# The order of a whole two-block transformer kernel, listed with another machine model of the framework

## Chip, cores and metric

One core of a Trainium2 chip. The metric is the device time of one execution in microseconds (us). Matmuls run on PE (with the weight loads, PEld, beside it), elementwise work on DVE, ACT and POOL; SP issues most of the loads from memory.

## What is computed

Two transformer blocks over 256 tokens of width 1024, one after the other, in float32. Cut to what matters here:

```python
def first_block(x, mem, ...):
    h = rms_norm(x, mix_norm_pre)
    q, kc, vc, ksl, vsl, kw, vw, gt, pin, u, v = split(h @ w_in)
    mix = concat([nsa_mixer(q, kc, ...), pool_mixer(pin, ...), sgu_mixer(u, v, ...)]) @ w_out
    x = x + rms_norm(mix, mix_norm_post)
    x = x + rms_norm(memory_attention(rms_norm(x), rms_norm(mem), ...))
    return x + rms_norm(conv_ffn(rms_norm(x), w_up, conv_w, w_down))

def second_block(x, mem, ...):
    qkv, z, a_g, b_g, c_q, c_kv, k_idx, w_idx, ug = split(rms_norm(x, norm_mix) @ w_in)
    y_a = gdn_mixer(qkv, z, a_g, b_g, ...)      # gated delta rule: solves (I + A) sol = rhs, A strictly lower
    y_b = dsa_mixer(c_q, c_kv, k_idx, w_idx, ...)  # scores, top-k, attention over the chosen keys
    y_c = conv_mixer(ug, conv_dw, ...)          # 31-tap causal depthwise convolution, layer norm
    x = x + concat([y_a, y_b, y_c]) @ w_out
    x = x + memory_cross_attention(rms_norm(x), rms_norm(mem), ...)
    return x + square(relu(rms_norm(x) @ mlp_w1)) @ mlp_w2
```

## The kernel before

All activations stay on the core; the weights are streamed. A weight tile of 128x1024 (512 KB) is loaded on SP (`load_w`, L207), and split into a rounded high part on ACT (`wh`, L220) and a remainder on DVE in two halves (`wl`, L222; some tiles on POOL, L227 and L228). Each product is three matmuls (`mm3`, L232 to L234: high by high, high by low, low by high). Results lie in PSUM tiles of three tags: `tp` (four buffers), `cc` and `fl` (two each).

The stages follow each other in `build` (L1644): the mixers of block 1, 0 to 179 us of the profile; the attention to memory, 179 to 290; the convolutional FFN, 290 to 447, and its last product, to 491; the mixers of block 2, to 670; the cross attention, to 714; the MLP, to 893.

Two of these stages mix chains of small dependent steps with plain projections, called filler here, by Python generators that are run in turn (`weave`, L77, and `beside`, L97):

- Block 1. `nsa` (L655) works on two halves of the tokens, i = 0 and 1, with eight units in each: a score matmul L740 into `tp`, a bias and row minimum on DVE, an exponential on ACT, transposes L751, a copy, and the matmul with the values L762 into `cc`. The transposes of the result are L306. `fill1` (L780) gives the filler: the projections of the memory's keys and values (tiles `fl`), the pooling and the gating mixer. `w_out` (tiles `cc`) comes after all of it.
- Block 2. `gdn` (L1306) needs the inverse of a unit triangular matrix per head, which `tri_inverse` (L1366) builds: L1386 on DVE starts it from `ti_m` (POOL, L1385), and then six levels follow, each of them transposes L1380 (copied by ACT, L1381), matmuls L1395 (copied by ACT, L1396), matmuls L1401 and an update on DVE, L1402, for two halves i. `dsa` (L1407) has the second small chain: the keys and values (L1433, copied by ACT, L1435), scores L1465, a loop of MAX and MATCH_REPLACE on DVE (L1479, L1481) that finds the top-k, and a softmax (L1494 to L1512). `conv31` (L1520) is a chain of taps on DVE, one L1527 each, with nothing else to wait for than its input `yg`; `conv_silu` (L1078) has the taps L1086 of a shorter convolution, copied in by ACT L1084. `rest2` (L1250) and `fill2` (L1156) give the filler (tiles `fl`).

None of this fixes the order on the engines. The code hands its instructions to the framework's `TileContext`. When the context ends, the framework walks through a model of the machine and lists each engine's instructions in the order in which they become ready in that model; among ready ones the earlier in the code goes first. The list is the program: each engine works through it in that order. The model by default is the one with which the framework also computes values. The waits between engines, and the places of the table loads on ACT, follow from the list.

```python
x, hT, ss = ...                       # stages call weave / beside, e.g. L642:
weave((self.nsa(w1, x2, qT, kT, vsw, gate, mixT), NW), (self.fill1(hT, mixT, x2), FW))
```

The function that the change touches:

## Time and profile before

| | us |
|---|---|
| median of three runs | 893.49 |
| lowest and highest of them | 891.78, 899.03 |
| the profiled execution, its own time | 895.26 |
| its span on the core | 893.0 |
| mean granted clock of TensorE | 0.983 of full |

The span is the stretch that the profile's rows cover; 2.3 us of the execution lie around it. Times in rows count from the start of the span.

### The profile page before, as it was taken

What the parts mean: (1) busy time and instruction counts of PE and PEld (TensorE: products, weight loads), DVE (VectorE), ACT (ScalarE), POOL (GpSimd) and SP (SyncE); (2) the same over time, 40 slices, a digit from 0 to 9 for tenths busy, and PEclk for the clock granted to TensorE, in tenths of its full rate; (3) what the DMA queues carried; (4) which work ended last, traced back from release to release, by engine and by line L of the source; (5) the groups of instructions that cost most, each with busy time, mean ns of one, the idle gap of its engine ahead of it and who ended that gap; (6) DMA issues with size and microseconds to landing.
All of it is one profiled execution on the core that took longest, in us unless ns stands there. A gap on an engine that the chain in (4) does not pass through costs nothing.

```text
span 893.0 us, 15247 instructions
## 1 busy us (share of the span) xinstructions
PE 853.7 (96%) x5813; PEld 776.2 (87%) x5813; DVE 622.1 (70%) x1404; ACT 463.1 (52%) x805; POOL 118.0 (13%) x125
## 2 busy tenths in 40 slices
PE   8899999988999999999999997989999999999998
PEld 7798877888888999999988996878898999999996
DVE  5568765656557878877775799987666766666663
ACT  5346454545554656655554664656555534444442
POOL 1324101221110000000002312621142000000000
PEclk9989999999899999999999998999999999999999
DMA  8995223567343666765541652202153355666661
GB/s 256 278 285 170 72 76 117 163 190 236 119 156 117 200 212 211 226 191 181 189 139 57 201 150 96 88 1 95 28 162 95 105 180 174 186 186 190 187 188 70
DMA packets 41012, 138.94 MB, mean 156 GB/s; under 512 B 4851, under 2 KB 6292, under 8 KB 40940
## 3 DMA queue, kind: packets, MB, share of 16 engines
q1 hardware_dynamic: 37440, 130.49, 46.6%
q10 hardware_dynamic: 2988, 6.06, 2.2%
q0 software_dynamic: 512, 1.44, 0.9%
q8 instruction: 45, 0.74, 0.3%
q14 instruction: 27, 0.22, 0.1%
HBM read 136.00 MB, written 1.44 MB: 154 GB/s over the span
## 4 chain that ended last, share of the span: by engine, by line
PE 71%; DVE 16%; DMA 5%; ACT 4%; issue 3%; POOL 1%; ACTq 0%; SPq 0%; POOLq 0%; DVEq 0%
PE tp L234 8%; PE tp L233 8%; PE tp L232 8%; PE fl L232 6%; PE fl L233 5%; PE fl L234 5%; PE cc L234 4%; PE cc L233 4%; PE cc L232 4%; DVE wl L222 3%; DVE cv_y L1527 2%; DMA wr<-in_w_in_dram 2%; PE tp L331 1%; PE cc L762 1%; DMA srow<-in_srows_dram 1%
## 5 line engine op out<-in xcount | busy, mean ns | idle before, releaser
L222 DVE TENSOR_TENSOR wl<-wr,wh 128x512 fp32r<-128x512 f32 (+2 forms) x418 | 281.3, 696 | 130.2 <-ACT wh L220 128.2
L220 ACT ACTIVATE wh<-wr 128x1024 fp32r<-128x1024 f32 (+2 forms) x209 | 217.8, 1044 | 198.8 <-PE tp L233 87.7
L232 PE MATMUL tp<-thi,wh 128*128 128x256 f32 x784 | 222.8, 284 | 2.5 <-ACT wh L220 2.5
L234 PE MATMUL tp<-thi,wl 128*128 128x256 f32 x784 | 222.7, 284 | 0.2 <-DVE wl L222 0.2
L233 PE MATMUL tp<-tlo,wh 128*128 128x256 f32 x784 | 222.7, 284 | 0.0
L232 PEld LDWEIGHTS tp<-thi,wh 128*128 128x128 f32 x784 | 150.6, 192 | 4.0 <-ACT wh L220 2.7
L233 PEld LDWEIGHTS tp<-tlo,wh 128*128 128x128 f32 x784 | 150.5, 192 | 1.3
L234 PEld LDWEIGHTS tp<-thi,wl 128*128 128x128 f32 x784 | 150.6, 192 | 0.4 <-DVE wl L222 0.4
L228 POOL TENSOR_TENSOR wl<-wr,wh 128x1024 fp32r<-128x1024 f32 (+2 forms) x21 | 49.9, 2382 | 298.1 <-ACT wh L227 295.0
L227 ACT ACTIVATE ff_h<-ff_y 128x256 fp32r<-128x256 f32 x54 | 22.2, 416 | 45.0 <-PE fl L234 42.1
L232 PE MATMUL fl<-thi,wh 128*128 128x256 f32 x144 | 42.6, 296 | 0.8 <-ACT wh L227 0.7
L232 PE MATMUL cc<-wh,ff_h 128*128 128x512 f32 x108 | 42.4, 392 | 0.9 <-ACT ff_h L227 0.9
L983 DVE SCALAR_TENSOR_TENSOR ff_y<-tp,col,ff_y 128x255 f32<-128x255 f32 x88 | 42.0, 477 | 0.8 <-ACT ff_y L981 0.6
L234 PE MATMUL cc<-wh,ff_h 128*128 128x512 f32 x108 | 42.4, 393 | 0.0
L233 PE MATMUL cc<-wl,ff_h 128*128 128x512 f32 x108 | 42.2, 391 | 0.0
L234 PE MATMUL fl<-wh,ff_h 128*128 128x512 f32 x108 | 42.2, 391 | 0.0
L233 PE MATMUL fl<-wl,ff_h 128*128 128x512 f32 x108 | 42.2, 391 | 0.0
L232 PE MATMUL fl<-wh,ff_h 128*128 128x512 f32 x108 | 42.1, 390 | 0.0
L233 PE MATMUL fl<-tlo,wh 128*128 128x256 f32 x144 | 41.7, 290 | 0.0
L234 PE MATMUL fl<-thi,wl 128*128 128x256 f32 x144 | 41.7, 289 | 0.0
L227 ACT ACTIVATE wh<-wr 128x1024 fp32r<-128x1024 f32 (+3 forms) x23 | 22.5, 984 | 22.2 <-DMA wr<-in_w_in_a_dram 4.9
L228 DVE TENSOR_TENSOR ff_h<-ff_y,ff_h 128x256 fp32r<-128x256 f32 x54 | 22.5, 422 | 14.9 <-ACT ff_h L227 14.9
(523 smaller groups left out, 1822.7 us busy)
## 6 DMA issues: line engine op xcount, KB each, us to landing
wr<-in_mlp_w_dram SPq DMA_DIRECT2D x64, 512.0 KB, 3.6
wr<-in_w_up_dram SPq DMA_DIRECT2D x44, 512.0 KB, 3.7
wr<-in_w_in_dram SPq DMA_DIRECT2D x31, 512.0 KB, 4.5
wr<-in_w_down_dram SPq DMA_DIRECT2D x22, 512.0 KB, 4.3
wr<-in_w_out_dram SPq DMA_DIRECT2D x16, 512.0 KB, 3.6
grow<-in_rows_dram ACTq DMA_DIRECT2D x8, 512.0 KB, 6.1
wr<-in_w_mk_dram SPq DMA_DIRECT2D x8, 512.0 KB, 3.6
wr<-in_w_mv_dram SPq DMA_DIRECT2D x8, 512.0 KB, 3.6
```

What stands on the lines that cost most here:

```text
L220: nc.scalar.activation(hi, raw, AF.Copy)
L222: nc.vector.tensor_tensor(lo[:, q], raw[:, q], hi[:, q].bitcast(F32), op=ALU.subtract)
L227: nc.scalar.activation(hi, raw, AF.Copy)
L228: (eng or nc.vector).tensor_tensor(lo, raw, hi.bitcast(F32), op=ALU.subtract)
L232: nc.tensor.matmul(out, a[0], b[0], start=first, stop=False)
L233: nc.tensor.matmul(out, a[0], b[1], start=False, stop=False)
L234: nc.tensor.matmul(out, a[1], b[0], start=False, stop=last)
L331: nc.tensor.matmul(pt[:, j * P:(j + 1) * P], xg[n][:, j * P:(j + 1) * P], dg, start=True, stop=True)
L762: nc.tensor.matmul(out[:, h * 64:(h + 1) * 64], pT[:, (e * (i + 1) + b) * P:(e * (i + 1) + b + 1) * P], vsw[b][:, vo:vo + 64], start=(b == ...
L983: nc.vector.scalar_tensor_tensor(y[:, e, k:], a[:, :S - k], self.c("conv_w", 44 * (2 - k) + c), y[:, e, k:], op0=ALU.mult, op1=ALU.add)
L1527: nc.vector.scalar_tensor_tensor(y[:, c, k:], yg[:, c, :S - k], self.c("conv_dw", 2 * (30 - k) + c), y[:, c, k:], op0=ALU.mult, op1=ALU.add)
```

## The change

One argument. The list of every engine is now made with the framework's timeline model of the machine in place of its model that computes values. No line that issues an instruction is edited.

```diff
-    with _tile.TileContext(nc) as tc:
+    with _tile.TileContext(nc, schedule_with_timeline_sim=True) as tc:
```

What the program holds is the same: 5351 instructions of PE with its waits left aside, 1388 of DVE, 128 of POOL and 260 of SP, each with the same operands. ACT has two more table loads, 20 for 18, since they stand wherever the next function needs another table. On PE nothing moves in the FFN (290 to 446 us) and nothing after the first 20 us of the MLP. The largest moves are in the mixers of block 1 (up to 41 us of the profile before) and of block 2 (up to 20 us).

Three places are shown. The first is DVE in the mixers of block 2, just ahead of the start of the triangular inverse, L1386 (`ds_cur` is the top-k loop's score tile, `cv_y` the sum of the convolution's taps). Before:

```order
L1474 TENSOR_TENSOR ds_cur_5876<-ds_cur_5876,con 128x128
L1086 SCALAR_TENSOR_TENSOR kq_5402<-fl_5944,col,kq_5402 128x255
L1229 SCALAR_TENSOR_TENSOR bq_1084_5927<-tp_6016,gd_dd_5922,t_1030_5711 128x128
...
L1086 SCALAR_TENSOR_TENSOR kq_5402<-fl_5944,col,kq_5402 128x253
L1479 MAX ds_m_1102_6032<-ds_cur_6030 128x8
L1386 TENSOR_TENSOR t_1030_5711<-con,ti_m_6044 128x512
L1481 MATCH_REPLACE ds_cur_6034<-ds_m_1102_6032,ds_cur_6030 128x128
L1386 TENSOR_TENSOR t_1030_5711<-con,ti_m_6053 128x512
```

The same place now:

```order
L1527 SCALAR_TENSOR_TENSOR cv_y_5401<-yg_5273,col,cv_y_5401 128x226
L1086 SCALAR_TENSOR_TENSOR kq_5402<-fl_5944,col,kq_5402 128x253
L1535 TENSOR_SCALAR cv_y_5401<-cv_y_5401,col 128x256
L1086 SCALAR_TENSOR_TENSOR vT_5403<-fl_6090,col,vT_5403 128x255
...
L1229 SCALAR_TENSOR_TENSOR bq_1084_5927<-tp_6025,gd_dd_5922,t_1030_5711 128x128
L1386 TENSOR_TENSOR t_1030_5711<-con,ti_m_6044 128x512
...
L1386 TENSOR_TENSOR t_1030_5711<-con,ti_m_6053 128x512
L1444 TENSOR_SCALAR ds_k_5557<-cc_5844,col 64x256 x2
L1453 TENSOR_SCALAR ds_sv_5858<-cc_5853 128x8
```

Now all 60 taps L1527 stand ahead of L1386, before 36 of them did, and the top-k loop, which had begun ahead of it, follows it.

The second place is PE in the same stage, from the start of the triangular inverse on (`fl_6262` is filler). Before:

```order
L1380 MATMUL tp_6056<-con,t_1030_5711 128x128 x4
L1395 MATMUL tp_6076<-t_1030_5711,ti_m_6074 128x128 x4
L1395 MATMUL tp_6084<-t_1030_5711,ti_m_6082 128x128 x4
L1401 MATMUL tp_6169<-t_1030_5711 128x128 x4
L1401 MATMUL tp_6175<-t_1030_5711 128x128 x4
L233 MATMUL fl_6262<-tlo_5075,wh_6265 128x256
...
L1395 MATMUL tp_6252<-t_1030_5711,ti_m_6250 128x128 x4
L233 MATMUL fl_6262<-tlo_5075,wh_6296 128x256
```

The same place now:

```order
L1442 MATMUL cc_5844<-con,ds_kn_5848 128x128
L1451 MATMUL cc_5853<-con,ds_pr_5798 128x2 x4
L1380 MATMUL tp_6047<-con,t_1030_5711 128x128 x4
...
L1401 MATMUL tp_6175<-t_1030_5711 128x128 x4
L1380 MATMUL tp_6181<-con,t_1030_5711 128x128 x4
L1380 MATMUL tp_6187<-con,t_1030_5711 128x128 x4
L1395 MATMUL tp_6244<-t_1030_5711,ti_m_6242 128x128 x4
L1395 MATMUL tp_6252<-t_1030_5711,ti_m_6250 128x128 x4
L1401 MATMUL tp_6334<-t_1030_5711 128x128 x4
L1401 MATMUL tp_6340<-t_1030_5711 128x128 x4
```

The filler `fl_6262` now stands ahead of and within the first level, and from the second level on the steps of the inverse follow each other with none between them. The keys of the second chain (L1442, L1451) stood well ahead before and now stand right in front of L1380.

The third place is PE in block 1, at the first units of the second half of the tokens (`fl_1374` is filler, `pr` the probabilities of a unit, `pT` their transposes). Before:

```order
L740 MATMUL tp_1300<-kT_483,qT_344 128x512
L729 MATMUL cc_1291<-vblk_790,pcT_1289 128x512
L234 MATMUL fl_1374<-t_166_958,wl_1409 128x256
...
L740 MATMUL tp_1352<-kT_483,qT_344 128x512
L751 MATMUL tp_1302<-con,pr_1301 128x128 x2
L232 MATMUL fl_1374<-t_166_958,wh_1408 128x256
...
L762 MATMUL cc_1299<-vsw_87_572,pT_1316 128x64
L751 MATMUL tp_1354<-con,pr_1353 128x128 x2
L232 MATMUL fl_1374<-t_166_958,wh_1408 128x256
```

The same place now:

```order
L740 MATMUL tp_1300<-kT_483,qT_344 128x512
L729 MATMUL cc_1291<-vblk_790,pcT_1289 128x512
L751 MATMUL tp_1302<-con,pr_1301 128x128 x2
L740 MATMUL tp_1352<-kT_483,qT_344 128x512
...
L762 MATMUL cc_1299<-vsw_87_572,pT_1316 128x64
L751 MATMUL tp_1354<-con,pr_1353 128x128 x2
L740 MATMUL tp_1438<-kT_483,qT_344 128x512
L751 MATMUL tp_1354<-con,pr_1353 128x128 x2
```

All of the filler now stands ahead of these eight units, beside the units of the first half; only 24 matmuls of `w_out` stand among the last three.

On SP, the three remaining loads of `t_36` (L581, 512 KB each) now stand ahead of the weight tiles `wr_384` and `wr_421` of the first projections; before, one of them stood between these two tiles and the other two behind them.

## Rows read from the trace of the kernel before

**Rows 1.** The page's first part: busy time, share of the span, instructions.

```profile
PE 853.7 (96%) x5813; PEld 776.2 (87%) x5813; DVE 622.1 (70%) x1404; ACT 463.1 (52%) x805; POOL 118.0 (13%) x125
```

**Rows 2.** Windows by stage: length, busy PE, PEld, DVE, ACT, POOL, clock, DMA share, GB/s.

```profile
0.00:67.00 67.00, 58.80 (x410) 53.58 (x411) 37.49 (x91) 29.44 (x52) 15.09 (x36) 0.93 0.90 273
67.00:179.00 112.00, 108.81 (x674) 91.11 (x674) 76.09 (x210) 59.73 (x134) 22.13 (x29) 1.00 0.39 120
179.00:245.00 66.00, 60.61 (x400) 55.37 (x399) 38.57 (x71) 34.87 (x66) 10.45 (x12) 0.92 0.55 183
...
513.00:536.00 23.00, 23.00 (x176) 22.11 (x175) 22.95 (x49) 14.06 (x22) 3.21 (x2) 1.00 0.53 154
536.00:558.00 22.00, 16.27 (x113) 15.07 (x112) 20.23 (x68) 9.19 (x21) 5.20 (x3) 0.84 0.29 94
558.00:580.00 22.00, 20.37 (x169) 19.46 (x168) 21.98 (x70) 13.07 (x23) 15.03 (x11) 1.00 0.25 91
580.00:603.00 23.00, 20.36 (x158) 17.95 (x157) 20.72 (x66) 12.87 (x28) 4.79 (x4) 1.00 0.00 1
603.00:650.00 47.00, 44.41 (x350) 40.18 (x349) 34.52 (x104) 25.82 (x55) 4.95 (x3) 1.00 0.21 68
...
670.00:714.00 44.00, 41.52 (x305) 38.10 (x305) 32.49 (x93) 24.35 (x50) 6.44 (x3) 0.96 0.33 99
714.00:893.00 179.00, 175.03 (x1115) 159.04 (x1113) 110.34 (x184) 72.59 (x93) 0.00 (x0) 1.00 0.56 170
```

**Rows 3.** Windows of DVE alone in the mixers of block 2: length, busy, clock, DMA.

```profile
513.00:550.00 37.00, 36.95 (x88) 0.91 0.48 149
550.00:565.70 15.70, 13.91 (x54) 1.00 0.11 35
```

**Rows 4.** Windows of PE alone: triangular inverse to the matmul L1298, and behind.

```profile
564.50:605.90 41.40, 37.82 (x305) 1.00 0.11 39
605.90:620.80 14.90, 14.35 (x115) 1.00 0.30 106
```

**Rows 5.** The taps: DVE's groups by line, 513 to 565.8 us.

```profile
L1527 DVE SCALAR_TENSOR_TENSOR cv_y<-yg,col,cv_y 128x252 f32<-128x252 f32 (+17 forms) x36 | 22.5, 659 | 0.0
```

**Rows 6.** Timeline of DVE: start, duration; taps, then the inverse's start and updates.

```profile
542.21 0.45 DVE L1527 SCALAR_TENSOR_TENSOR cv_y<-yg,col,cv_y 128x239 f32<-128x239 f32 x1
542.59 0.47 DVE L1086 SCALAR_TENSOR_TENSOR kq<-fl,col,kq 128x254 f32<-128x254 f32 x1
...
563.55 0.91 DVE L1386 TENSOR_TENSOR t<-con,ti_m 128x512 f32<-128x512 f32 x1
...
564.64 1.31 DVE L1386 TENSOR_TENSOR t<-con,ti_m 128x512 f32<-128x512 f32 x1
...
571.43 0.66 DVE L1402 SCALAR_TENSOR_TENSOR t<-tp,t 128x512 f32<-128x512 f32 x1
...
620.04 0.69 DVE L1402 SCALAR_TENSOR_TENSOR t<-tp,t 128x512 f32<-128x512 f32 x1 [0.20 <-PE tp L1401]
```

**Rows 7.** Timelines of PE and ACT about 545 us; brackets: idle before, and releaser.

```profile
545.19 0.79 PE L1433 MATMUL cc<-ds_wkv,ckT 128*128 128x128 f32 x2 [5.72 <-ACT ds_v L1435]
...
543.86 0.47 ACT L1084 ACTIVATE kq<-fl,col 128x256 f32<-128x256 f32 x1 [6.47 <-DVE kq L1086]
```

**Rows 8.** Timeline of ACT about a table load.

```profile
612.22 1.28 ACT L1502 ACT_TABLE_LOAD   x1
613.51 0.51 ACT L1502 ACTIVATE ds_pr<-sS,nm 128x256 f32<-128x256 f32 x1
```

**Rows 9.** Second half of the units in block 1: the window, and PE behind the last.

```profile
107.00:147.00 40.00, 38.91 (x258) 31.12 (x256) 25.63 (x74) 17.87 (x46) 5.56 (x5) 1.00 0.26 81
...
143.71 0.48 PE L232 MATMUL fl<-wh,t 128*128 128x512 f32 x1
...
146.54 0.63 PE L306 MATMUL tp<-con,oa 128*128 128x128 f32 x4 [0.97 <-DVE oa L778]
```

**Rows 10.** The page's waits: PE in the first 67 us.

```profile
PE tp L232 <- ACT wh L220: 2.5, 1, 2.5
```

## Prediction

> **What bounds the kernel now.** I read the page's busy shares first, then the windows by stage, then in the stages with idle PE the waits and the timelines. The page shows PE busy for 853.7 of 893.0 us [rows 1]; 39 us of idle PE, and what the clock loses behind it, are all that an order can win. The windows say where it lies [rows 2]. From 714 us on PE is busy 175.0 of 179 us, and nothing moves there but in its first 20 us. The idle time is at the start (67.0 less 58.8 is 8.2 us, with the DMA engines busy for 0.90 of it at 273 GB/s, so this stage is set by loads), in 179 to 245 us (5.4 us), and above all in the mixers of block 2: 536 to 558 us has 5.7 us of idle PE and a granted clock of 0.84, 558 to 580 has 1.6, 580 to 603 has 2.6 and 603 to 650 has 2.6.
>
> In these mixers DVE is the bound, not PE. It was busy 36.95 of 37.0 us from 513 to 550, 13.9 of 15.7 to 565.7 [rows 3], 21.98 of 22 in 558 to 580 and 20.7 of 23 in 580 to 603 [rows 2]. The longest single wait of PE shows it: L1433 waited 5.72 us for ACT, which itself sat 6.47 us behind an L1084 that waited for the taps L1086 on DVE [rows 7]. So what counts in this stage is what stands ahead of what on DVE.
>
> **The mixers of block 2: +3 us, between -4 and +11.** The 60 taps of conv31 feed only the layer norm at the stage's end. Before, 36 of them ran by 565.8 us [rows 5]; now all 60 stand ahead of the first L1386. A tap costs DVE 0.38 us from its start to the next one's [rows 6], so 24 more make 9.1 us. Against them, rows of the top-k chain (L1444, L1453, L1471 to L1481 and a reciprocal root) have left that place, and some splits L222, the steps L1535 and taps L1086 have come to it; adding up all rows of DVE ahead of L1386 in both lists, each at its own duration less the 0.07 us by which neighbours overlap [rows 6], the net is 8.7 us. The 1.8 us that DVE was idle in 550 to 565.7 [rows 3] may be filled by it: L1386 comes 6.9 to 8.7 us later. It started at 563.55 before, so at 570.5 to 572.2, and its second half ends not before 565.95 + 6.9 = 572.9.
>
> PE waits for that. It was at this place at 564.5 [rows 4], and has by my count of the list 1.9 us more filler ahead of it now. At L1433 it is relieved a little: some eight filler matmuls (0.13 us each, as 176 matmuls fill 23.0 us in 513 to 536 [rows 2]) and a small group more stand in front of its wait, while kq's taps are where they were (their place in DVE's sum is moved by less than 1 us), so about 1.5 us of the 5.7 are covered. Since the next wait is for DVE, that gain goes into it. PE is at L1380 by about 566 and waits for L1386 (and, just ahead, for the keys of L1442, whose steps on DVE have moved back by more still) for 5 to 6 us.
>
> From there the two lists have the same work up to L1298, where PE stood at 605.9. PE's share of it is 37.8 us [rows 4], less the 1.9 already done: 566 + 5.5 + 35.9 = 607.4. But from the second level of the inverse on no filler is left between its steps, and each level has DVE's update and ACT's two copies in it that PE must sit out in part; I put 0.4 us on each of four levels, so 609, +3 against 605.9. The lower end: the first level, from the end of L1386 to the end of L1402, took 572.09 - 565.95 = 6.1 us with both halves in flight [rows 6]; the other five took 48.6 us together, 9.7 each, since taps and top-k rows stood between the updates on DVE. If all levels now took 6.1, the inverse would end at 572.9 + 6 x 6.1 = 609.5 where it ended at 620.7; PE's work of the stretch does not allow all of that, since 52.2 us of it (37.8 and 14.4 [rows 4]) less 1.9 from 566 on end at 616.3: -4. The upper end: the same 9.7 us per level behind the late start, 572.9 + 6.1 + 48.6 = 627.6, is +7; and behind a wait of 5 us the clock may be lowered, as it was after the 5.7 us of L1433, when the stretch of 22 us had 0.84: 0.16 of 22 is 3.5 us. Together +11. I take +3, near the count of PE's work, as PE is nearly full in this stretch.
>
> **The second half of block 1's units: 0, between -4 and +6.** In 107 to 147 us PE is busy 38.9 of 40 [rows 9], because filler stands between the units. Taking it out ahead moves work and saves none; the gain can be the 3.2 us that PE is idle in 67 to 179 [rows 2] and a little of the changes between kinds of matmul, -4. What is exposed: eight units, each with an exponential and a copy that PE waits for. No row shows such a unit without filler. Two units in flight may cover each other, which costs nothing; the nearest row is the wait of the transposes L306 behind the last unit, 0.97 us with filler ahead of them [rows 9], so up to about 1 us a unit; I take 0.5, 4 us in all. And L306 loses its cover, the filler from 143.7 to about 145.6 [rows 9], 1.9 us more. That is +6 if the filler brought nothing earlier. I take the middle of -4 and +6, rounded down to 0, since the filler does run dense in front.
>
> **The start: +1, between -1 and +4.** Three loads of 512 KB stand ahead of two weight tiles that PE waits for. At 273 GB/s [rows 2] each takes 1.9 us. PE's wait of 2.5 us [rows 10] for the second tile grows by two loads, 3.8 us, at the most; but these loads must be done in this stage in any order, and what comes behind them comes as much earlier. So the most of it is given back by 67 us.
>
> **Elsewhere: +2, between -2 and +5.** In 179 to 245 us a load's release is put behind other splits on DVE, and in 670 to 714 two sums of heads stand ahead of the matmuls of the next product that covered them; PE has 2.5 us of idle time there already [rows 2]. One microsecond each. The moves in 245 to 290 and 447 to 513 exchange a wait ahead of the transposed norms for one behind them, 0.
>
> **The two more table loads: 0.** A load takes 1.28 us on ACT, and the next function starts at once, at 613.51 after 612.22 + 1.28 = 613.50 [rows 8]. ACT is busy 25.8 of 47 us in 603 to 650 [rows 2], where they fall, so it has room; if both stood in a chain it were 2.6 us, which the range holds.
>
> The Trainium skill, "ScalarE: Activation LUTs", section "What ACT_TABLE_LOAD costs", gives about 1283 ns for the load and about 1380 ns of draining beside it, 2.66 us for a switch. The first figure agrees with the row; of the second this row shows nothing, as the next activation began 0.01 us after the load's end. By the page two switches would cost up to 5.3 us in place of 2.6; the sum stays as it is.
>
> **The sum** is 3 + 0 + 1 + 2 + 0 = 6 us, on an execution of 895.3 us: 901.3. That execution lies 1.8 us above the median of the three runs, so the forecast for the median is 893.5 + 6 = 899.5 us.
>
> **Rivals.** First, the change is a gain: with the taps gone early, the inverse's levels run at 6.1 us, -4 in block 2; the filler of block 1 in front brings its 4, the start 1 and the rest stays as it is: -9, 884.5 us. For it speaks that DVE has no idle time to lose in 513 to 550 and that the taps do stand in the way of the updates later; against it that PE has its own work to do there. Second, the change is a loss, because what covered the chains is spent ahead of them: PE waits for L1386, the clock falls behind that wait, and the bare levels take 9.7 us as before, +11; the bare units of block 1 give 6 by the same mechanism; with the start and the rest as forecast, +3, that is +20, 913.5 us. It is decided at L1380, 566 us, and takes over as soon as L1386 comes more than 3 us later than the filler in front of it lasts. For it speaks that DVE's sum ahead of L1386 is a lower bound; against it that top-k rows have left the later part. Third, the list differs and the time does not: waits move by a few us each and are caught up at the next full stretch, 893.5 us; this is part of my forecast's case, as a measurement of this kernel cannot tell 1% (8.9 us) from nothing.
>
> **How the numbers follow.** I give 0.45 to the forecast's case (with the third rival in it), 0.20 to the gain and 0.35 to the loss, whose terms are more and larger. The range takes in the gain with 5 us beyond it and the loss with 2.5: 879 to 916. The likeliest case's own range is 886 to 902.
>
> **What would show it.** Right: in the profile after, the first L1386 starts 7 us later behind a full DVE, PE waits 5 us or more at L1442 or L1380, the levels are shorter than 9.7 us, and FFN and MLP take as long as before. Wrong: no wait of PE at that place, or L1386 at its old time; an idle DVE between 513 and 550; or a change of more than 5 us in a stage where I put 2 or less.

## The result, and the profile after

After the change the kernel takes 929.94 us (median of four runs, 929.04 to 933.13) where before took 892.63: a ratio of 1.0424, interval 1.039 to 1.0458. That is 37 us slower. The forecast was 899.5 us, and its range ended at 916.

The profiled execution took 933.13 us, its span is 931.2. The page's first part answers to [rows 1]:

```profile
PE 867.4 (93%) x5813; PEld 790.2 (85%) x5813; DVE 632.3 (68%) x1404; ACT 467.2 (50%) x807; POOL 120.2 (13%) x125
```

PE is idle for 63.8 us where it was for 39.3, and busy for 13.7 us longer with as many instructions. The second number is the clock. The view of the cores gives a mean granted clock of 0.960 for 0.983. The granted clock has two levels, full and half, so the time at half is (1 - 0.960) x 2 x 931.2 = 74 us where it was (1 - 0.983) x 2 x 893.0 = 30 us. The windows by stage, with the columns of [rows 2], cut at the same matmuls as there where the text compares them:

```profile
0.00:74.00 74.00, 62.30 (x410) 56.65 (x411) 38.66 (x95) 31.02 (x56) 15.32 (x38) 0.86 0.82 258
74.00:115.00 41.00, 37.47 (x274) 34.34 (x274) 29.55 (x96) 21.61 (x52) 11.44 (x18) 0.91 0.34 112
115.00:170.00 55.00, 50.68 (x308) 40.73 (x306) 31.13 (x85) 23.74 (x58) 4.89 (x5) 1.00 0.27 88
170.00:195.00 25.00, 22.71 (x93) 18.08 (x93) 14.42 (x20) 11.43 (x17) 3.12 (x3) 0.87 0.33 105
...
550.00:572.00 22.00, 18.72 (x126) 17.91 (x124) 22.00 (x59) 14.42 (x26) 5.81 (x3) 0.84 0.41 134
572.00:600.00 28.00, 16.25 (x112) 15.83 (x112) 27.14 (x73) 8.72 (x15) 12.71 (x9) 0.82 0.19 60
600.00:630.00 30.00, 26.95 (x203) 25.13 (x204) 18.40 (x64) 15.33 (x35) 6.45 (x6) 0.89 0.05 18
630.00:665.00 35.00, 28.68 (x196) 24.95 (x196) 25.92 (x87) 21.55 (x42) 3.62 (x2) 0.90 0.10 31
...
752.00:931.00 179.00, 175.16 (x1117) 159.18 (x1115) 110.53 (x185) 72.94 (x93) 0.00 (x0) 1.00 0.54 168
```

Read the first and the last row first: the first 410 matmuls took 74 us in place of 67, and the MLP takes the same 179 us. The units of block 1 (74 to 195 us) have 10.1 us of idle PE where [rows 2] had 3.2. In the mixers of block 2, DVE is still full to 600 us (27.1 of 28), and then it is not: 18.4 of 30 us, in a stretch in which PE is not full either. That is what a chain of small steps with little beside it leaves.

The same matmul can be found in both traces, and the difference of its two start times says how late PE is at that place. By stages, worked out as medians over each stretch:

| stage (time before) | PE late at its end, us | the stage's own part |
|---|---|---|
| start (to 67) | 7.0 | +7.0 |
| units of block 1 (to 179) | 16.8 | +9.8 |
| memory and FFN (to 513) | 13.8 | -3.0 |
| mixers of block 2 (to 670) | 34.7 | +20.9 |
| cross attention (to 714) | 38.1 | +3.4 |
| MLP (to 893) | 38.1 | 0 |

The waits of PE, from the list of what it waited for (us in total, times, longest):

```profile
PE cc L1442 <- DVE ds_kn L1441: 8.9, 1, 8.9
PE tp L232 <- ACT wh L220: 8.4, 2, 6.8
PE cc L1505 <- ACT ds_pr L1502: 6.4, 3, 3.9
PE tp L1380 <- DVE t L1402: 5.5, 4, 3.6
PE cc L1433 <- ACT ds_qi L1423: 3.0, 1, 3.0
...
PE tp L725 <- ACT sc L722: 2.2, 1, 2.2
...
PE tp L306 <- DVE oa L778: 1.6, 1, 1.6
PE tp L751 <- ACT pr L748: 1.6, 4, 1.1
```

Three of the first four stand in the mixers of block 2. The timeline of DVE there (start, duration) shows the start of the inverse and its first level, against [rows 6]:

```profile
585.01 0.67 DVE L1386 TENSOR_TENSOR t<-con,ti_m 128x512 f32<-128x512 f32 x1
586.67 1.56 DVE L1386 TENSOR_TENSOR t<-con,ti_m 128x512 f32<-128x512 f32 x1
...
599.72 0.67 DVE L1402 SCALAR_TENSOR_TENSOR t<-tp,t 128x512 f32<-128x512 f32 x1
...
602.16 0.68 DVE L1402 SCALAR_TENSOR_TENSOR t<-tp,t 128x512 f32<-128x512 f32 x1
```

L1386 starts 21.5 us later than before, of which 13.8 us are the stage's later begin: 7.7 us. And the first level takes 602.84 - 588.23 = 14.6 us, not 6.1. The matmul L1298, to which the prediction counted, stood at 605.94 us before and now starts here:

```profile
633.34 0.60 PE L1298 MATMUL fl<-con,kq 128*128 128x128 f32 x4
```

That is 27.4 us later, 13.6 by the stage's own part.

The largest wait, L1442, looks back at a place that the prediction named only in passing. The keys of the sparse attention need a reciprocal root, some ten tiny instructions on DVE from L1436 to L1441 (tiles `dsk_`). Before, that stretch took 3.8 us:

```profile
546.97 0.15 DVE L1436 TENSOR_SCALAR ds_ss<-ds_ss 128x2 f32<-128x2 f32 x1
...
550.75 0.34 DVE L1441 TENSOR_SCALAR ds_kn<-cc,dsk_y 128x128 f32<-128x128 f32 x1
```

Now it is this:

```profile
564.05 0.16 DVE L1436 TENSOR_SCALAR ds_ss<-ds_ss 128x2 f32<-128x2 f32 x1
...
573.03 2.29 DVE L258 TENSOR_TENSOR dsk_t<-dsk_y 128x2 f32<-128x2 f32 x1
...
580.23 0.34 DVE L1441 TENSOR_SCALAR ds_kn<-cc,dsk_y 128x128 f32<-128x128 f32 x1
```

16.2 us. What stands between, by DVE's groups of this stretch in the trace of after, and then of before (busy us, mean ns):

```profile
L1527 DVE SCALAR_TENSOR_TENSOR cv_y<-yg,col,cv_y 128x234 f32<-128x234 f32 (+8 forms) x17 | 7.3, 445 | 0.0
L222 DVE TENSOR_TENSOR wl<-wr,wh 128x512 fp32r<-128x512 f32 x6 | 3.8, 680 | 0.0
...
L1086 DVE SCALAR_TENSOR_TENSOR kq<-fl,col,kq 128x255 f32<-128x255 f32 (+2 forms) x5 | 2.3, 469 | 0.0
L1086 DVE SCALAR_TENSOR_TENSOR vT<-fl,col,vT 128x255 f32<-128x255 f32 (+2 forms) x3 | 1.4, 464 | 0.0
```

```profile
L1527 DVE SCALAR_TENSOR_TENSOR cv_y<-yg,col,cv_y 128x236 f32<-128x236 f32 (+2 forms) x4 | 1.8, 455 | 0.0
L250 DVE TENSOR_SCALAR gdr_y<-gd_ss 128x8 int32<-128x8 int32 x1 | 1.1, 1070 | 0.0
L1086 DVE SCALAR_TENSOR_TENSOR kq<-fl,col,kq 128x253 f32<-128x253 f32 x1 | 0.5, 470 | 0.0
```

Seventeen taps for four, eight L1086 for one, six splits L222 for none. Each is work that no one on the chain waits for. PE's wait for these keys reaches the inverse too: the matmuls L1228 that stand behind L1442 start at 580.89 us, the last steps L1229 on DVE that use them at 583.71 and 584.49, and POOL waits 2.17 us for L1229 before the second `ti_m`, which the second L1386 needs.

### The profile page after: what moved, and what is told of

Its sections match the earlier page's. It is cut to its first block, busy times and chain, and to the rows that moved or that the text cites. A ratio compares the mean times of both kernels' runs of the same rounds, so it can differ in the third digit from the quotient of the medians.

```text
span 931.2 us, 15245 instructions
## 1 busy us (share of the span) xinstructions
PE 867.4 (93%) x5813; PEld 790.2 (85%) x5813; DVE 632.3 (68%) x1404; ACT 467.2 (50%) x807; POOL 120.2 (13%) x125
## 4 chain that ended last, share of the span: by engine, by line
PE 77%; DVE 11%; ACT 4%; DMA 4%; issue 2%; POOL 1%; SPq 1%; ACTq 0%; DVEq 0%; POOLq 0%
PE tp L233 9%; PE tp L234 9%; PE tp L232 9%; PE fl L232 6%; PE fl L233 6%; PE fl L234 6%; PE cc L232 5%; PE cc L233 4%; PE cc L234 4%; DVE wl L222 2%; DMA wr<-in_w_in_dram 2%; PE tp L930 2%; DVE cv_y L1527 2%; PE tp L740 1%; ACT wh L220 1%
## 5 line engine op out<-in xcount | busy, mean ns | idle before, releaser
L222 DVE TENSOR_TENSOR wl<-wr,wh 128x512 fp32r<-128x512 f32 (+2 forms) x418 | 275.0, 700 | 126.3 <-ACT wh L220 123.1
L220 ACT ACTIVATE wh<-wr 128x1024 fp32r<-128x1024 f32 (+2 forms) x209 | 217.9, 1044 | 209.6 <-PE tp L233 85.3
L232 PE MATMUL tp<-thi,wh 128*128 128x256 f32 x784 | 224.0, 286 | 8.4 <-ACT wh L220 8.4
L232 PEld LDWEIGHTS tp<-thi,wh 128*128 128x128 f32 x784 | 151.6, 194 | 10.2 <-ACT wh L220 8.8
L228 POOL TENSOR_TENSOR wl<-wr,wh 128x1024 fp32r<-128x1024 f32 (+2 forms) x21 | 50.4, 2404 | 324.1 <-ACT wh L227 324.1
L232 PE MATMUL fl<-thi,wh 128*128 128x256 f32 x144 | 43.6, 303 | 0.1
L232 PE MATMUL cc<-wh,ff_h 128*128 128x512 f32 x108 | 42.4, 392 | 0.5 <-ACT ff_h L227 0.5
L232 PE MATMUL fl<-wh,ff_h 128*128 128x512 f32 x108 | 42.1, 390 | 0.0
L228 DVE TENSOR_TENSOR ff_h<-ff_y,ff_h 128x256 fp32r<-128x256 f32 x54 | 22.5, 422 | 16.4 <-ACT ff_h L227 16.4
```

Of the source, the lines that this page charges most:

```text
L220: nc.scalar.activation(hi, raw, AF.Copy)
L222: nc.vector.tensor_tensor(lo[:, q], raw[:, q], hi[:, q].bitcast(F32), op=ALU.subtract)
L228: (eng or nc.vector).tensor_tensor(lo, raw, hi.bitcast(F32), op=ALU.subtract)
L232: nc.tensor.matmul(out, a[0], b[0], start=first, stop=False)
```

## The experiments

All of them set the order of instructions and nothing else, except two that add matmuls. One function ties each engine's instructions together in a given list, without a wait:

```python
def pin(tc):
    by = {i.name: i for i in tc.nc.cur_bb.bb.instructions}
    info = mybir.DependencyInfo(mybir.DependencyClass.NoSync, mybir.DependencyReason.DATA)
    for text in PINNED:
        row = [x for x in text.split() if "I-" + x in by]
        for a, b in zip(row, row[1:]):
            tc.add_manual_dep(by["I-" + b], "I-" + a, info, reason="pin")
```

In the diffs `A` and `B` are the lists of all engines after and before, and `put(A, B, lo, hi)` is A with the instructions numbered lo to hi in B's order. The numbers are those of the code: up to 579 the start, to 1949 the units of block 1 and their filler, to 5189 memory and FFN, to 7290 the mixers of block 2. Each kernel is compared with runs of before on the same chip (891.7 to 893.2 us by group). Where no number of runs is given, there were two, or four of the cuts, up to 6.6 us apart.

**Which stage.** First the whole list, then one stage each set back.

```diff
-PINNED = A
+PINNED = B
```

> The argument of the change is in, and all lists are held in the order that they had before. Theory: only the order counts, so this is the kernel before, 893 us within 0.5%. Rival: the argument changes something beside the order (waits, placing of tiles): over 900 us.

892.09 us (eight runs), ratio 0.9996 (0.9967 to 1.0026). So the order is the cause: what else the argument does is worth 0.3% at the most.

```diff
-PINNED = A
+PINNED = put(A, B, 5190, 7290)
```

> The new list, but with the mixers of block 2 (all engines) held in the order that they had before. Theory: the loss is made of parts that belong to the lists of single stages; between 550 and 665 us the lag of PE behind the kernel before grows from 13.8 to 34.8 us, so this kernel takes 930 - 21 = 909 us, and its PE has no wait over 6 us in that stage. Rival (the loss there is handed on from the earlier stages, through the phase in which TensorE's clock falls): the stage stays slow with its old list, over 918 us.

908.82 us: 21 us come back.

```diff
-PINNED = A
+PINNED = put(A, B, 580, 1949)
```

> The new list, but with the units of block 1 and the filler beside them, up to w_out, held in the order that they had before. Theory: the lag grows there from 7 to 15.5 us, so 930 - 8.5 = 921 us. Rival: as these units' chain is short anyway and what costs is the late start of the stage behind its loads, 927 us or more.

917.61 us (914.33 and 920.89): 12.3 come back. The profile shows how: in the window of the same units, PE and the clock are what they were.

```profile
74.00:115.00 41.00, 38.96 (x291) 34.58 (x291) 33.60 (x113) 21.96 (x56) 12.02 (x18) 1.00 0.38 124
115.00:155.00 40.00, 38.91 (x235) 30.26 (x234) 24.71 (x68) 18.81 (x46) 4.46 (x4) 1.00 0.28 88
```

The clock of 0.91 of the same 41 us in after is gone together with waits of 1 to 2 us (L725, L306, L751, L762): some of the 12 us is the clock's.

```diff
-PINNED = A
+PINNED = put(A, B, 1, 579)
```

> The new list, but with the start, up to the units of block 1, held in the order that it had before. Theory: the lag of 7 us at 67 us comes from the three loads of t_36 ahead of two weight tiles and is not given back, so 930 - 7 = 923 us. Rival (my prediction's reasoning: the loads must be done in this stage in any order, so the lag is given back later): 928 us or more.

931.11 us: nothing comes back in the medians, against 7.0 us in the profile of after. The start was also tried alone in the kernel before, with SP's loads only:

```diff
-PINNED = B
+PINNED = B, but SP by put(B, A, 1, 579)
```

> The lists of the kernel before, with the new order on SP alone in the start: three loads of t_36 ahead of the tiles wr_384 and wr_421. Theory (SP's order is the start's loss): PE waits 7 us for wr_384 as in the changed kernel, lag of PE at 62 to 70 us 2.5 to 7 us, 895 to 900 us in all. Rival (it is given back by 67 us, or the order of ACT costs it): lag under 1.5 us there.

900.30 us, ratio 1.0101 (1.0058 to 1.0144): 8.6 us slower. The two results contradict each other as a sum. In both starts that are late, loads land late: in after, ACT waits 9.18 us for a weight tile that was issued at 21.33 us and landed at 36.37, 15 us behind its issue, where before it took 7.5 us (14.45 to 21.94). With SP's loads alone the tile behind it takes 12.9 us (17.13 to 30.01, before 21.90 to 30.48), but PE's long wait, 8.2 us, is at L1011 for DVE and not for a weight tile as expected. And the profile of the kernel with the start set back (931.11 us) still has a wait of 7.6 us at L232 for L220. What the start's list costs therefore stays open between 0 and 9 us.

The reverse for the mixers: the kernel before with their new order alone.

```diff
-PINNED = B
+PINNED = put(B, A, 5190, 7290)
```

> The lists of the kernel before, with the mixers of block 2 alone in the new order. Theory (the stages' losses add up): 893 + 21 = 914 us, the lag between 550 and 665 us grows by 19 to 22 us. Rival (the loss needs the shifted phase of the clock from the stages before): under 908 us.

910.91 us, ratio 1.0204 (1.0153 to 1.0255): 19 us. With 21 from the other side the stage's price is 19 to 21 us.

**Single pieces of the mixers.** Each of the next five takes one suspect.

```diff
+L1527 x18
 L1386
 ...
-L1527 x18
```

> The lists of the kernel before, with one thing moved: the 18 taps L1527 that stood behind the first L1386 on DVE are put ahead of it. Theory (the taps' place is the cause of the mixers' loss): 18 x 0.38 us = 6.9 us of DVE work, less 1.8 us of idle DVE, make L1386 5 us later, PE waits as long at L1380 and its clock falls behind the wait; +6 to +12, 899 to 905 us. Rival (the taps that come ahead are gone from between the inverse's levels, which run faster by as much, so it is the rest of the list that costs): within 3 us of the kernel before.

896.61 us, ratio 1.0043 (1.0011 to 1.0075). In the kernel before, the late taps ahead of L1386 cost 4 to 5 us (6.3 in the profile's stage), between the two expectations. L1386 moved from 563.55 to 568.50 us, and as PE is 2.7 us earlier at 513 in this profile, that is 7.7 us later by the stage's own part, as in after. PE took waits of 2.9 us at L232 for the taps L1086 and 2.2 us at L1228 for L1229, and none at L1380 for L1386. So a late L1386 with the keys in time costs some quarter of the stage's loss.

```diff
-L1527 x18, L1535 x2
 L1386
 ...
+L1527 x18, L1535 x2
```

> The new lists, with the taps of the convolution alone put back on DVE, each behind as many other instructions of the stage as before: 31 then stand ahead of the first L1386, not 60. Theory (the taps): 11 us of DVE work leave the place in front of L1386, the wait of 8.9 us at L1442 goes and the stage regains most of its 21 us: 915 us or less. Rival (the filler spent ahead on PE and the late top-k chain cost it): 925 us or more, with PE's waits moved to the levels and to L1505.

930.14 us: nothing comes back, though 42 taps stand ahead of L1386 again, as before (and not 31, as the expectation has it). The taps alone were not it, and the trace says why. With only 5 taps left in it, the stretch from L1436 to L1441 still takes 15.7 us, since the L222 stand there, and now wait for ACT (busy us, mean ns, idle before and for whom):

```profile
L222 DVE TENSOR_TENSOR wl<-wr,wh 128x512 fp32r<-128x512 f32 x6 | 3.9, 686 | 3.0 <-ACT wh L220 3.0
L1086 DVE SCALAR_TENSOR_TENSOR kq<-fl,col,kq 128x255 f32<-128x255 f32 (+2 forms) x5 | 2.4, 471 | 0.0
L1527 DVE SCALAR_TENSOR_TENSOR cv_y<-yg,col,cv_y 128x236 f32<-128x236 f32 (+2 forms) x5 | 2.3, 457 | 0.0
```

Next, the thirteen rows of the top-k chain that stand between L1386 and the first L1402:

```diff
+L1402 x2
 L1471, L1473 x3, L1474, L1479 x4, L1481 x4
-L1402 x2
```

> The new lists, with DVE's first pair of updates L1402 put ahead of the 13 rows of the top-k chain (L1471 to L1481) that stood in front of them. Theory (the first level of the inverse took 14.6 us, not 6.1, since PE's results waited on DVE behind the top-k chain, from 596.9 to 599.7 us, and PE then 3.6 and 1.3 us for it): the waits at L1380 go, 4 to 6 us less, 924 to 926 us. Rival (the top-k chain, now later, brings its softmax later, and the waits at L1505 grow by as much): 929 us or more.

933.45 us: nothing. The first level takes 10.6 us for 14.6; the pair, moved from 599.72 and 602.16 to 597.58 and 599.78, waits for PE, which has a new wait:

```profile
PE tp L1401 <- ACT t L1396: 4.6, 2, 4.5
```

Then the clock, with 18 matmuls whose result is not used, ahead of L1442. The first try put them ahead of its second instruction, where PE does not wait; the second try ahead of the first.

```diff
             kn = self.t([P, 2, 64], "ds_kn", bufs=1)
             nc.vector.tensor_scalar(kn, ...)
+            for _ in range(18 * (1 - i)):
+                nc.tensor.matmul(pt[:, S:], self.ident, self.con[:, :S], start=True, stop=True)
             nc.tensor.transpose(pt[:, i * P:(i + 1) * P], ...)
```

> The new lists, with 18 matmuls more on PE, 128x128 by 256 columns, into unused columns of a tile, just ahead of the L1442 for which PE waited 8.9 us; their product is not used. They need some 8 us that PE had waited anyway. Theory (a good part of the loss is the clock, at half for 10.2 us behind this wait): the clock stays at full level there, -3 to -5 us, 925 to 927 us. Rival (DVE sets the pace there, so a faster PE brings nothing): 929 to 931 us.

With `18 * i`, 935.83 us, 6 us more, as PE is held up by them and its wait stays at 8.9 us. It says nothing on the clock.

> The new lists, with 18 matmuls more on PE (128x128 by 256 columns, into unused columns of a tile, product not used), now ahead of the first L1442, where the wait of 8.9 us is; before they stood ahead of the second one, where PE waited for nothing. They take some 7 us of that wait. Theory (the clock at half behind the wait is part of the loss): the stretch of 10.2 us at half goes, and the time falls by 2 to 5 us, to 925 to 928 us. Rival (DVE sets the pace up to the first L1402 in any case): within 1 us of 930.

933.06 us (929.78 to 936.34): no gain. The half clock behind that place lasted 3.4 us in place of 10.2, the wait fell to 1.2 us, and yet the same two waits follow:

```profile
PE cc L1507 <- ACT ds_pr L1504: 6.4, 3, 3.9
PE tp L1380 <- DVE t L1402: 5.6, 4, 3.7
```

(L1507 is L1505 behind two added lines.) Against the profile of after PE is 3.4 us earlier ahead of the stage and 3.4 us behind it, so the stage takes as long as there. In this stretch the chain sets the pace, not PE.

**Where in the mixers.** No single piece gives the time back, and all together do. So the list was cut: one order up to an instruction, and what is then left in the other. `cut(X, Y, i)` is the stage in X's order to instruction i, the rest in Y's.

```diff
-PINNED = put(B, A, 5190, 7290)
+PINNED = put(B, cut(B, A, L1386 second), 5190, 7290)
```

> Before, with the mixers of block 2 (alone) in before's order up to the second L1386, and what is then left of them in the order of after. The new order of the whole stage costs 19 us (e11). Theory (what was put ahead of L1386 sets the loss: taps, norms and front rows of the sparse attention): most is gone, 892 to 897 us. Rival (what was put behind it sets it: top-k rows, transposes and filler beside the levels): 902 to 911 us.

911.77 us, ratio 1.0221 (1.0176 to 1.0266): all of the loss is there, the rival held. But the timeline of ACT shows a cause that this mixture itself has made (start, duration; idle before, and releaser):

```profile
559.73 0.62 ACT L1088 ACTIVATE kq<-kq 128x512 f32<-128x512 f32 x1
575.24 0.47 ACT L1084 ACTIVATE vT<-fl,col 128x256 f32<-128x256 f32 x1 [14.89 <-DVE vT L1086]
...
578.45 0.58 ACT L1381 ACTIVATE t<-tp 128x512 f32<-128x512 f32 x1
```

ACT sits for 14.9 us in front of an L1084 that waits for taps on DVE, and L1381, which the inverse waits for, is listed behind it. Behind the inverse PE waits 6.4 us at L1505, as in after, though the keys are in time here (3.8 us from L1436 to L1441).

```diff
-PINNED = put(B, A, 5190, 7290)
+PINNED = put(B, cut(A, B, L1386 second), 5190, 7290)
```

> Before, with the mixers of block 2 in the order of after up to the second L1386, and what is then left in before's order. Theory (the part ahead of L1386 sets the loss): 905 to 911 us. Rival (the part behind it): 892 to 898 us. If each of e13 and e14 lies in the middle, both halves have a share, and the shares add up to 19 us.

900.48 us, ratio 1.01 (1.0053 to 1.0148): 7.3 us above its own runs of before. The two halves make 18.6 + 7.3 = 26 us, so they do not add up to 19. The keys are as late here as in after (16.1 us from L1436 to L1441, and the first level takes 12.6 us):

```profile
PE cc L1442 <- DVE ds_kn L1441: 9.4, 1, 9.4
```

Two more cuts, at the end of the first level:

```diff
-PINNED = put(B, A, 5190, 7290)
+PINNED = put(B, cut(B, A, L1402 second), 5190, 7290)
```

> As e13, but before's order goes on to the second instruction of L1402, the end of the first level. Theory: 892 to 896 us, and the inverse is not later than in before by more than 2 us. Rival (levels two to six lack filler in the new order): 898 to 908 us, with L1402 pairs 10 to 12 us apart instead of 7.

907.56 us, ratio 1.0172 (1.0114 to 1.023): the rival's time, with another reason. The first pairs of L1402 are 19 us apart, and the later ones 7 to 11, as in after. In the 19 us PE waits 6.3 us at L1401 for ACT, which again sits in front of an L1084; behind the inverse it waits 5.9 us at L1505, again with the keys in time (3.8 us).

```diff
-PINNED = put(B, A, 5190, 7290)
+PINNED = put(B, cut(A, B, L1402 second), 5190, 7290)
```

> As e14, but the order of after goes on to the second instruction of L1402, then before's order. Theory: 908 to 912 us, the whole loss of e11 (910.9). Rival (the levels behind it set the loss): 895 to 902 us.

906.72 us, ratio 1.016 (1.0116 to 1.0204): between the two. Behind the first level PE gets no later here (12.0 us at 604 to 612, 12.2 at 730 to 880), while with the new order throughout it loses another 7.6 us there, beside the wait at L1505. Is that a term of its own?

```diff
-PINNED = put(B, A, 5190, 7290)
+PINNED = put(B, cut(A, B, L1402 sixth), 5190, 7290)
```

> As e16, but the order of after goes on to the end of the third level of the inverse (the sixth instruction of L1402), then before's order, which puts the last rows of the sparse attention (L1505) ahead of the inverse's end. Theory (L1505 at the stage's end without cover is a separate term of 7.3 us): 902 to 906 us, with no wait at L1505 and a lag that stays flat behind the inverse. Rival (the time is lost in any case, as another wait takes its place): 909 to 912 us, as e11.

909.85 us, ratio 1.0209 (1.0171 to 1.0247): no. The wait at L1505 is 1.3 us for 6.4, and yet PE is 15.6 us late by 604 us and stays so. The waits at L1380 have grown only from 5.5 to 6.2 us, so they do not show where the time went instead. My theory fell, the rival's time came. The last cut lies ahead of the keys' reciprocal root:

```diff
-PINNED = put(B, A, 5190, 7290)
+PINNED = put(B, cut(A, B, L1433 second), 5190, 7290)
```

> Before, with the mixers of block 2 in the order of after up to the second instruction of L1433 on PE, then before's order: the 157 rows that after has between that and the first L1441 on DVE (68 in before) are not put ahead of it. Theory (this stretch, which holds up the norms and keys of the sparse attention, sets the loss of the front): 891 to 897 us, and the wait at L1442 under 3 us. Rival (the front was lost earlier, or PE's wait only moves on): 900 to 911 us, as e14 or more.

889.33 us (887.91 to 892.73, ten runs), ratio 0.9975 (0.9957 to 0.9994). All 19 us are gone. In the profiles the stage takes as long as in before: PE is 5.9 us earlier at 513 us and 6.0 behind the stage. So the 2.9 us below before are not the stage's: ahead of it the lists are the same, and eleven profiles with the same lists up to 179 us differ there by up to 5.8 us. The timeline of DVE and the waits of PE:

```profile
542.71 0.17 DVE L1436 TENSOR_SCALAR ds_ss<-ds_ss 128x2 f32<-128x2 f32 x1 [0.18 <-ACT junk L265]
...
545.95 0.34 DVE L1441 TENSOR_SCALAR ds_kn<-cc,dsk_y 128x128 f32<-128x128 f32 x1
```

```profile
PE cc L1505 <- ACT ds_pr L1502: 0.5, 1, 0.5
PE cc L1442 <- DVE ds_kn L1441: 0.4, 1, 0.4
```

From L1436 to L1441 it takes 3.2 us for 16.2, and both waits are gone. So the new order up to L1433 costs nothing; the loss is made by what is listed behind that instruction. Ahead of L1441 that is 156 rows on all engines for 67, and on DVE 59 for 25.

This does not show the late keys to be the whole cause, for everything behind is in before's order again too, and L1386 and its first level (6.1 us) are as in before. The cuts with after's order in front part the loss, by their ratios:

| after's order up to | ratio | more than the row above, us |
|---|---|---|
| second L1433 | 0.9975 | |
| second L1386 | 1.0100 | 11 |
| end of the first level | 1.0160 | 5 |
| end of the third level | 1.0209 | 4 |
| the whole stage | 1.0204 | 0 |

The rows with the keys, up to L1386, make some 11 of 20 us, and by the profiles 16 of 21 (PE loses 16.2 us in the stage with the new order up to L1386, 21.0 with all of it; the first profile is of the slowest of four executions, 904.03 us). With the keys just as late, the rest comes only when the new order goes on behind L1386. Which of the rows there cost it, and whether they would with the keys in time, stays open: the two kernels with before's order in front also lose 14 to 19 us, but in part by waits of ACT that the mixture makes. The new order of the whole stage with the keys' steps alone moved forward was not run.

**A version that beats both.** Memory and FFN were the one stage in which the new order gained.

```diff
-PINNED = B
+PINNED = put(B, A, 1950, 5189)
```

> The lists of the kernel before, with the new order in the attention to memory, the FFN and what is projected beside them (block 1's second part) alone, where the lag fell in the changed kernel. Theory (the new list is better there: the lag fell by 3.0 us from 160 to 556 us in the changed kernel and by 5.6 us where its first stages were held in the old order): 3 to 5 us less than before, 888 to 890 us. Rival (it fell because a late kernel finds its loads ready): within 1 us of before.

887.45 us (886.61 to 889.84, twelve runs) against 891.89, ratio 0.9949 (0.9929 to 0.997). In the window 179 to 245 of [rows 2] the clock was 0.92; now:

```profile
179.00:245.00 66.00, 61.64 (x424) 56.25 (x423) 38.34 (x69) 37.06 (x69) 12.75 (x12) 1.00 0.53 179
```

and PE's wait at L948 is 1.1 us for 3.0, with a new one of 2.2 us at L930. By the profiles PE gains 4.3 us in this stage. The same with the list of the 889.33 us kernel in the mixers was not run. Moving PE's filler alone in the mixers was not tried.

## Why the prediction was wrong

**What bounds the kernel.** Right: in the mixers DVE is the bound, and what counts is what stands ahead of what on it. The waits appeared where this says, at L1442 and L1380, and FFN and MLP take as long as before.

**The mixers, +3 forecast, +19 to +21 measured.** L1386 comes 7.7 us later by its own part of the stage, within the 6.9 to 8.7 forecast. My count of the taps had an error that cancelled itself: I read 36 taps in a window that began at 513 us, but six had run ahead of it; so 18 taps moved and not 24, while the net of 8.7 us was summed from the lists' rows and held. In part that is luck, as the last steps ahead of L1386 also waited for PE behind L1442, which the sum leaves out. PE's wait there was forecast at 5 to 6 us and is 8.9.

The step that failed is the sentence behind it, "From there the two lists have the same work up to L1298". From it the forecast had PE at L1298 3 us later, and nothing lost behind; measured are 13.6 us at L1298 by the stage's own part, and 7.3 more behind it. The step treats the inverse as the only chain, and takes the keys of L1442, "whose steps on DVE have moved back by more still", as another reason for the same wait. They are the head of a second chain. L1441 is 29.5 us later than before, 15.7 by its own part of the stage, and with it come the scores, the top-k loop and the softmax. So rows of that chain that I had booked as gone from the front (L1444, L1453, a reciprocal root, L1471 to L1481) stand between L1386 and the first L1402 on DVE, and the first level, on which my sum put nothing, takes 14.6 us for 6.1. The later levels take 6.9, 6.9, 7.3, 10.3 and 10.7 us: three lie between the 6.1 and 9.7 of the prediction, two above, and together they are shorter than before (42.1 for 48.6 us). At the end the softmax (L1505) has nothing beside it and PE waits 6.4 us, a term that my sum did not have.

How far the cause is shown: the order of the rows between L1433 and the second L1386, the keys among them, makes 11 of 20 us by the times and 16 of 21 by the profiles, and a late L1386 with the keys in time only 4 to 6. That the later part follows from the keys is argued and not shown, and for the wait at L1505 two runs speak against it, as it stays with the keys in time.

My rival of a loss had the right sign, and a chance of 0.35, but the wrong place and price: it was to be decided at L1380 and by the inverse. Its condition ("L1386 comes more than 3 us later than the filler in front of it lasts") was met, and would have given 913.5.

The clock, put only into the upper end (3.5 us), falls in this stage to 0.82 to 0.90 over 93 us. Yet the added matmuls show that giving back 6.8 us of half clock at the longest wait gains nothing while the chain is late: a mark of the loss at that place, not its cause.

**Block 1, 0 forecast, +10 to +12 measured.** The bound of 1 us a unit was fair: the new waits at L725, L306, L751, L762 and L729 make some 9 us (2.2 + 1.6 + 1.2 + 1.6 + 1.2 + 0.7 + 0.8). What failed is the choice of the middle: filler in front was to give back what bare units lose. PE had only 3.2 us of idle time there to win [rows 2], and the bare units cost the clock too (0.91 and 0.87 in two of the windows), which I had not counted.

**The start, +1.** The wait of 2.5 us at L232 became 8.4 us in two; "the most of it is given back by 67 us" was wrong in the profile (7.0 us late there), and is open in the medians, as told.

**Elsewhere, +2.** Memory and FFN gained 3.0 us in the profile, 4.4 when changed alone, where I put +1; the cross attention lost 3.4 where I put +1. The parts that runs price (21, 12 and -4) make 29 of the 37 us; the other 8 fall on the start and the cross attention, and are not parted by any run. **The table loads, 0**: no wait of PE shows them.

## What to carry to other kernels

When a list puts independent work in front of a small step, don't ask only how late that step gets, but which chain it heads, and follow that chain to where it meets the next one on the same engine. Here the single repairs (taps, top-k rows, clock) gave nothing. Cuts of the list by time, one order up to an instruction and the other from there, found at the sixth where the loss begins; but a cut sets back everything behind it, and may make waits of its own, so it finds a place and not yet a cause. And a new order need not be taken whole: stage by stage it lost 19 to 21 us in one and gained 4 in another.

## What was not expected of the hardware

Two tiny instructions of DVE lasted until the instruction of POOL beside them ended. L258 on 128x2 numbers took 2.29 us, from 573.03 to 575.32, where it takes 0.15 us otherwise; POOL's timeline has in the same stretch:

```profile
572.81 2.50 POOL L228 TENSOR_TENSOR wl<-wr,wh 128x1024 fp32r<-128x1024 f32 x1 [10.67 <-ACT wh L227]
```

It ends at 575.31. In the trace before, L250 took 1.07 us, from 547.45 to 548.52, beside POOL's L1214, from 547.40 to 548.49. Not all do so: there L1546, on 128x1 numbers, took 0.15 us at 621.49 within a POOL instruction L228 that ran from 619.66 to 622.02. The Trainium skill, "SBUF — State Buffer", section "Who interferes with whom", says that a DVE instruction with two inputs in SBUF contends with a POOL instruction that reads SBUF, and that the later one is blocked for the whole of the other, and that a tensor_scalar can be held up in its two-port modes; the rows of L258 (two inputs) and of L250 (a TENSOR_SCALAR) agree; whether L250 ran in such a mode no row shows. Here 2.3 of the 16.2 us of the chain were of this kind. No run took it apart, so what it costs the kernel is not shown.

An execution of this kernel spends 74 us at the lower clock in place of 30, in stretches of 3 to 10 us. Giving back 6.8 of them gained nothing at one place; what all of them cost no run shows, as the lower clock went only together with the waits.
